# Moving the stores of a streaming rotary-embedding kernel from ScalarE's DMA ring to SyncE's ring of loads, with the later loads placed one slab later

## The chip, the cores and the metric

The kernel runs on one core of one Trainium2 chip. The metric is device microseconds of that core, the median of several executions. A span is the time from the first to the last event of one profiled execution; the reported time is about 2 us longer (162.8 against a span of 160.8 for the kernel before).

## The reference, cut to what matters

```python
batch, seq, dim, num_heads = 16, 512, 1024, 16
x = x.reshape(batch, seq, num_heads, head_dim)            # f32
x1, x2 = x[..., :half_dim], x[..., half_dim:]
rotated = np.concatenate([x1 * cos - x2 * sin,
                          x1 * sin + x2 * cos], axis=-1)  # f32
```

Each element is read once and written once: 33.5 MB in, 33.5 MB out.

## The kernel before

The input is cut into eight slabs of 4 MiB (128 partitions x 8192 f32). Five slab buffers hold loads, and results are written back into the same buffers. A slab is worked on in two halves ("passes"): ScalarE casts a half to bf16 (below: a cast in), VectorE makes two products and a sum, ScalarE casts the result back to f32 in the slab (a cast back), and the finished slab is stored. Loads are issued by SyncE (SP), stores by ScalarE; a DMA ring is the queue of transfers that one of these engines has issued.

```python
def load(s):
    slab[s] = slabs.tile([P, W], f32, tag="slab", name="slab")
    nc.sync.dma_start(out=slab[s], in_=dram(x, s))
...                                   # load(0) to load(4), tables
def cast(u):
    s, k = u
    xb[u] = tpool.tile([P, PW], bf16, tag="xb", name="xb")
    nc.scalar.copy(out=xb[u], in_=view(slab[s], k * PW, (1, PW)))

passes = [(s, k) for s in range(nslabs) for k in range(rpp // rows)]
cast(passes[0])
for i, u in enumerate(passes):
    if i + 1 < len(passes):
        cast(passes[i + 1])           # one pass ahead
    s, k = u
    xs, xu = slab[s], xb.pop(u)
    t2 = t2pool.tile([P, PW], bf16, tag="t2")
    ...                               # VectorE: t2 = xu*sin, xu = xu*cos, xu += swapped t2
    nc.scalar.copy(out=view(xs, k * PW, (1, PW)), in_=xu)
    if k == rpp // rows - 1:
        nc.scalar.dma_start(out=dram(out_flat, s), in_=xs)
        if s + slots < nslabs:
            load(s + slots)
```

The order in this text is not the order on the engines. A scheduler fixes each engine's order when the kernel is built, from its own estimate of when data will be there; the engines then keep to it: in the profile after, ScalarE idles 3.55 us before its cast back at 87.37, although the last packet of slab 5's load had ended at 81.55 and its cast in stands next in the order.

## Time and profile before

| | before |
|---|---|
| time | 162.81 us (162.44 to 162.89) |
| span of the profiled run | 160.8 us |
| ScalarE busy, VectorE busy | 114.8 us, 111.3 us |
| DMA rate over the span | 418 GB/s, 420 to 438 in the stages from 4 to 146.7 us |
| store 7 issued, last byte landed | 146.70, 159.94 us |

In the page's part 2 the span is cut into 40 slices of 4.02 us, and each digit is the busy share of a slice in tenths. A DMA row that is all nines, with engines that are 70% busy, tells that the transfers set the pace. The last slab, in the timeline (columns: start, length, engine, line, operation, and in brackets the idle time before it and what ended it; ACTq and SPq are the engines' DMA issues):

```profile
125.38 3.60 ACT L117 CAST xb<-slab 128x4096 bf16<-128x4096 f32 x1 [5.13 <-DMA slab<-in_x_dram]
128.89 3.60 ACT L137 CAST slab<-xb 128x4096 f32<-128x4096 bf16 x1
...
143.06 3.60 ACT L137 CAST slab<-xb 128x4096 f32<-128x4096 bf16 x1 [3.46 <-DVE xb L133]
146.70 0.34 ACTq L139 DMA_DIRECT2D out_dram<-slab  x1
```

The cast back at 128.89 is slab 6's: ScalarE begins slab 7 before it has finished slab 6.

### The profile page before, as it was taken

What the parts mean: (1) busy time and instruction counts of PE and PEld (TensorE: products, weight loads), DVE (VectorE), ACT (ScalarE), POOL (GpSimd) and SP (SyncE); (2) the same over time, 40 slices, a digit from 0 to 9 for tenths busy, and PEclk for the clock granted to TensorE, in tenths of its full rate; (3) what the DMA queues carried; (4) which work ended last, traced back from release to release, by engine and by line L of the source; (5) the groups of instructions that cost most, each with busy time, mean ns of one, the idle gap of its engine ahead of it and who ended that gap; (6) DMA issues with size and microseconds to landing.
All of it is one profiled execution on the core that took longest, in us unless ns stands there. A gap on an engine that the chain in (4) does not pass through costs nothing.

```text
span 160.8 us, 182 instructions
## 1 busy us (share of the span) xinstructions
PE 0.6 (0%) x4; PEld 0.4 (0%) x4; DVE 111.3 (69%) x52; ACT 114.8 (71%) x33; POOL 2.3 (1%) x9
## 2 busy tenths in 40 slices
PE   0010000000000000000000000000000000000000
PEld 0000000000000000000000000000000000000000
DVE  0003799999999999999997599907997099950000
ACT  3006939899999999999984999069990899744000
POOL 5000000000000000000000000000000000000000
DMA  6999999999999999999999999999999999999993
GB/s 220 448 408 399 473 432 399 473 432 318 416 432 456 408 432 456 416 432 456 416 432 456 416 424 440 440 416 432 456 408 432 465 408 432 456 416 432 456 416 171
DMA packets 2368, 67.24 MB, mean 418 GB/s; under 512 B 288, under 2 KB 288, under 8 KB 320
## 3 DMA queue, kind: packets, MB, share of 16 engines
q1 hardware_dynamic: 1152, 33.55, 49.4%
q10 hardware_dynamic: 1152, 33.55, 48.3%
q0 software_dynamic: 64, 0.13, 0.2%
HBM read 33.69 MB, written 33.55 MB: 418 GB/s over the span
## 4 chain that ended last, share of the span: by engine, by line
DMA 47%; ACT 25%; DVE 13%; issue 6%; ACTq 0%; SPq 0%
DMA slab<-in_x_dram 25%; DMA out_dram<-slab 22%; ACT slab L137 16%; ACT xb L117 9%; DVE xb L133 4%; DVE t L130 4%; DVE xb L130 4%; ACTq L137 0%; SPq L65 0%
## 5 line engine op out<-in xcount | busy, mean ns | idle before, releaser
L117 ACT CAST xb<-slab 128x4096 bf16<-128x4096 f32 x16 | 57.5, 3602 | 27.1 <-DMA slab<-in_x_dram 27.1
L137 ACT CAST slab<-xb 128x4096 f32<-128x4096 bf16 x16 | 57.6, 3603 | 4.1 <-DVE xb L133 3.9
L130 DVE TENSOR_TENSOR t<-xb,tab 128x4096 bf16<-128x4096 bf16 x16 | 36.7, 2291 | 18.8 <-ACT xb L117 18.4
L133 DVE TENSOR_TENSOR xb<-xb,t 128x4096 bf16<-128x4096 bf16 x16 | 36.7, 2292 | 0.5
L130 DVE TENSOR_TENSOR xb<-xb,tab 128x4096 bf16<-128x4096 bf16 x16 | 36.7, 2292 | 0.5
L92 DVE CAST tab<-raw 128x256 bf16<-128x256 f32 x1 | 0.3, 294 | 11.1 <-DMA raw<-in_sin_dram 11.1
L117 ACT ACT_TABLE_LOAD x1 | 1.3, 1283 | 0.7 <-PEq L158 0.7
L102 DVE CAST tab<-acc 128x512 bf16<-128x512 f32 x1 | 0.7, 692 | 0.7 <-PE acc L96 0.7
L75 POOL DMA_DIRECT2D raw<-in_cos_dram x1 | 0.7, 674 | 0.8 <-POOLq L158 0.8
L96 PE MATMUL acc<-tab,pick 128*128 128x128 bf16 x4 | 0.6, 302 | 11.5 <-DVE tab L92 11.5
L87 POOL TENSOR_SCALAR_AFFINE_SELECT pick<-pick 128x128 bf16<-128x128 bf16 x2 | 0.5, 290 | 0.1
L75 POOL DMA_DIRECT2D raw<-in_sin_dram x1 | 0.5, 537 | 0.0
L96 PEld LDWEIGHTS <-pick 128*128 128x128 bf16 x4 | 0.4, 128 | 11.4 <-issue 8.2
L104 DVE CAST tab<-acc 128x256 bf16<-128x256 f32 x1 | 0.4, 416 | 0.0
L106 DVE TENSOR_SCALAR tab<-acc 128x256 bf16<-128x256 f32 x1 | 0.4, 414 | 0.0
L84 POOL MEMSET pick<- 128x256 bf16 x1 | 0.3, 330 | 0.0
L158 POOL MEMSET const-float32-0.0<- 128x1 f32 x1 | 0.1, 100 | 0.2 <-issue 0.2
L158 POOL MEMSET const-bfloat16-1.0<- 128x1 bf16 x1 | 0.1, 103 | 0.0
L158 POOL MEMSET const-uint8-127<- 128x1 uint8 x1 | 0.1, 103 | 0.0
L158 POOL MEMSET const-float32-1.0<- 128x1 f32 x1 | 0.1, 100 | 0.0
## 6 DMA issues: line engine op xcount, KB each, us to landing
slab<-in_x_dram SPq DMA_DIRECT2D x8, 4096.0 KB, 27.1
out_dram<-slab ACTq DMA_DIRECT2D x8, 4096.0 KB, 28.9
raw<-in_cos_dram POOLq DMA_DIRECT2D x1, 64.0 KB, 7.1
raw<-in_sin_dram POOLq DMA_DIRECT2D x1, 64.0 KB, 9.1
```

Of the source, the lines that this page charges most:

```text
L75: nc.gpsimd.dma_start(out=view(raw, i * TR * half, (1, TR * half)), in_=bass.AP(tensor=src.tensor, offset=src.offset, ap=[[TR * half, P], ...
L84: nc.gpsimd.memset(pick, 0.0)
L87: nc.gpsimd.affine_select(out=part, in_=part, compare_op=mybir.AluOpType.not_equal, fill=1.0, base=-g, pattern=[[0, P // SP], [-G, SP]], c ...
L96: nc.tensor.matmul(view(acc, i * TW + g * TR * half, (1, TR * half)), view(pick, g * P, (1, P)), view(tab1, i * TR * half, (1, TR * half)) ...
L102: nc.vector.tensor_copy(out=view(tab, 0, (hd, 2 * rpp), (1, half)), in_=view(acc, 0, (half, 2 * rpp), (1, half)))
L104: nc.vector.tensor_copy(out=view(tab, half, (hd, rpp), (1, half)), in_=view(acc, 0, (half, rpp), (1, half)))
L106: nc.vector.tensor_scalar_mul(out=view(tab, rpp * hd + half, (hd, rpp), (1, half)), in0=view(acc, TW, (half, rpp), (1, half)), scalar1=-1.0)
L117: nc.scalar.copy(out=xb[u], in_=view(slab[s], k * PW, (1, PW)))
L130: nc.vector.tensor_mul(out=t, in0=xu, in1=view(tab, a + k * rows * hd, (hd, rows), (0, nh), (1, hd)))
L133: nc.vector.tensor_add(out=xu, in0=xu, in1=view(t2, half, (hd, rows * nh), (-half, 2), (1, half)))
L137: nc.scalar.copy(out=view(xs, k * PW, (1, PW)), in_=xu)
L158: nc = _bacc.Bacc("TRN2", target_bir_lowering=False, num_devices=1)
```

## The change

The intent is one hardware ring for both directions: five loads, two stores, then a load and a store by turns, then the last stores. As a ring is served in order, a load would never have to share the DMA engines with a store. To make this possible each later load is placed one slab later, so that SyncE, which issues in order, is not held up by a load whose buffer is not yet free.

```diff
         nc.scalar.copy(out=view(xs, k * PW, (1, PW)), in_=xu)
         if k == rpp // rows - 1:
-            nc.scalar.dma_start(out=dram(out_flat, s), in_=xs)
-            if s + slots < nslabs:
-                load(s + slots)
+
+            nc.sync.dma_start(out=dram(out_flat, s), in_=xs)
+            if s >= 1 and s - 1 + slots < nslabs:
+                load(s - 1 + slots)
```

## The prediction

> **What bounds the kernel now.** I first read the page's parts 1 and 2, to see whether an engine or the transfers fill the span. No compute engine does; the DMA engines do.
>
> ```profile
> PE 0.6 (0%) x4; PEld 0.4 (0%) x4; DVE 111.3 (69%) x52; ACT 114.8 (71%) x33; POOL 2.3 (1%) x9
> DMA  6999999999999999999999999999999999999993
> GB/s 220 448 408 399 473 432 399 473 432 318 416 432 456 408 432 456 416 432 456 416 432 456 416 424 440 440 416 432 456 408 432 465 408 432 456 416 432 456 416 171
> HBM read 33.69 MB, written 33.55 MB: 418 GB/s over the span
> ```
>
> Only the first and the last slice (4.02 us each) are not full. The table of windows says the same by stage (columns: window, length, busy time of PE, PEld, DVE, ACT, POOL with counts, clock, DMA share, GB/s):
>
> ```profile
> 4.00:34.40 30.40, 0.59 (x4) 0.32 (x3) 18.81 (x12) 17.85 (x6) 0.00 (x0) 1.00 0.99 428
> 62.80:98.20 35.40, 0.00 (x0) 0.00 (x0) 31.61 (x15) 32.61 (x10) 0.00 (x0) 1.00 1.01 435
> 125.40:146.70 21.30, 0.00 (x0) 0.00 (x0) 13.75 (x6) 17.80 (x5) 0.00 (x0) 1.00 1.02 438
> ```
>
> The first window holds loads alone, the second loads and stores, the third mostly stores. The rate is 428 to 438 GB/s in all, so it depends neither on direction nor on whether one ring or two are active. In the packet records of the trace a 32 KiB packet takes a median of 1.213 us in either queue, and one slab (4 MiB, 8 packets on each of 16 DMA engines) therefore 8 x 1.213 = 9.70 us. Neighbouring loads 1, 2, 3 begin 9.72 and 9.71 us apart, stores 5, 6, 7 9.69 apart: a border between two transfers of one ring costs nothing that can be seen. Sixteen slabs are 155.3 us of a span of 160.8. The kernel before is bound by its transfers, and what compute waits for is mostly them (the list of waits: 27.1 us of ScalarE for loads).
>
> The chain of waits ends in ScalarE's last cast and the last store, but that is not the slack to watch: at 146.7, when store 7 is issued, the ring still held part of store 6, so the DMA engines did not starve. What matters is the timeline of the compute engines, because it says how long they would need without waiting:
>
> ```profile
> 13.50 7.11 ACT L117 CAST xb<-slab 128x4096 bf16<-128x4096 f32 x2 [11.48 <-DMA slab<-in_x_dram]
> 17.14 2.29 DVE L130 TENSOR_TENSOR t<-xb,tab 128x4096 bf16<-128x4096 bf16 x1 [3.67 <-ACT xb L117]
> ...
> 28.39 2.29 DVE L133 TENSOR_TENSOR xb<-xb,t 128x4096 bf16<-128x4096 bf16 x1
> ...
> 30.77 3.60 ACT L137 CAST slab<-xb 128x4096 f32<-128x4096 bf16 x1 [0.45 <-DVE xb L133]
> ...
> 76.82 3.60 ACT L117 CAST xb<-slab 128x4096 bf16<-128x4096 f32 x1
> ...
> 80.33 3.60 ACT L137 CAST slab<-xb 128x4096 f32<-128x4096 bf16 x1
> ...
> 85.11 2.29 DVE L133 TENSOR_TENSOR xb<-xb,t 128x4096 bf16<-128x4096 bf16 x1
> 86.67 3.60 ACT L117 CAST xb<-slab 128x4096 bf16<-128x4096 f32 x1 [2.74 <-DMA slab<-in_x_dram]
> ```
>
> Two rhythms are to be seen. Slab 0 has nothing beside it and runs casts, VectorE, casts back one after the other: 13.50 to 30.77 + 3.60 = 34.37, which is **20.87 us for a slab on its own**. From there to 76.82, ScalarE takes turns (cast in of the next half slab, cast back of this one) and a slab costs 4 x 3.5 = 14.2 us (stores issued at 34.41, 48.59, 62.77, 76.95): **14.18 us for a slab that overlaps its neighbour**.
>
> **What the Trainium skill says.** "DMA: Bandwidth & Descriptors", section "Queues, rings and completion order": SP and ACT each own one row of rings on the same 16 DMA engines, each ring is consumed in order, and an engine goes round the rings packet by packet. The trace agrees: while both queues have work their 32 KiB packets alternate on an engine, each of 1.213 us, and a load that shares takes about 18 us from its first to its last packet where a lone one takes 10.4. Same page, "Issuing engines are not separate DMA queues": issuing from two engines at once saves only sequencer time. The trace agrees here: 428 GB/s with one queue, 435 with two. Same page, "Where 436 GB/s comes from": 435 GB/s as the ceiling; the 428 to 438 measured sit on it, so no ordering can make the transfers themselves faster.
>
> **The change part by part.**
>
> 1. *Removed*: eight store issues of about 0.34 us from ScalarE's queue. In the timeline these lie beside the running cast (ACTq 34.41 within ACT 34.29 to 37.89). Worth nothing.
>
> 2. *Moved*: loads and stores now share one first-in-first-out ring. The total of bytes and the rate stay, so I lay the ring out with 9.71 us for a slab, starting from load 0's landing at 13.48: loads 1 to 4 end at 23.2, 32.9, 42.6, 52.3; then stores 0 and 1 at 62.0 and 71.7; load 5 81.4; store 2 91.1; load 6 100.8; store 3 110.5; load 7 120.2; store 4 129.9; store 5 139.6; store 6 149.3. Is each in the ring by its turn? Load 5 waits for store 0 (62.3) and is due at 71.7. Store 2 is ready at 62.8, due at 81.4. Load 6 waits for store 1 (72.0), due at 91.1; load 7 waits for store 2 (91.5), due at 110.5. SP issues in program order and blocks at each wait, but no block lasts past the due time; the least margin of these is 9 us. Up to here the DMA engines never run dry.
>
> 3. *Moved without being in the diff*: the scheduler has another order on ScalarE. In the built program, loads 5, 6 and 7 are expected late, so from slab 4 on ScalarE no longer takes turns: it has both casts back of slab 4, then both casts in of slab 5, both back of slab 5, both in of slab 6, both back, both in of slab 7, both back. VectorE's order changes with it (t, mul, t, add, mul, add, just that of slab 0). Engines run in program order, so slab 6 cannot start before slab 5 has been cast back, though its data landed long before. Each of slabs 5, 6, 7 now has slab 0's rhythm, 20.87 us in place of 14.18: 3 x 6.7 = **20 us more of compute**, which the before kernel had as waiting for loads instead (first casts after 86.67, 106.03, 125.38).
>
> The compute chain, step by step. Up to ScalarE's 80.33 as before. VectorE's last add of slab 4 ends at 85.11 + 2.29 = 87.40; cast back 87.45 to 91.05; so store 4 is ready at 91.05 (due 120.2). Slab 5's first cast starts at 90.97 (casts follow each other by 3.5 us; its load landed at about 81.7, no wait). Its end: 90.97 + 20.87 = 111.84. Slab 6: from 111.74 to 132.61. Slab 7: from 132.51 to **153.4** (its load landed at 120.5, again no wait). Stores 5 and 6 are ready at 111.8 and 132.6, due at 129.9 and 139.6, in time. **Store 7 is due at 149.3 and ready at 153.4.** The ring is empty for 4 us plus the latency of a cold start.
>
> 4. *The end.* Store 7 starts with an empty ring. The one transfer that did so before, load 0, took 12.74 us from issue to landing (the chain of waits has it as its first DMA piece): 1.0 to the first packet, then slow first packets of 1.8 to 2.1 us, then 1.22 each. A bare 1.0 + 9.7 + 0.35 is 11.1. I take 12.0, an estimate between the two: 153.45 + 12.0 = 165.4. Before, the last landing was 0.9 us ahead of the end of the span (159.9 of 160.8), so the span is 166.3, and the reported time is 2.0 more (162.81 against 160.8): **168.3 us**, that is +5.5 us, or 3.4%. By the same sums, with 11.1 it is 167.4, with 12.74 169.1.
>
> 5. *Given back*: slice 10 of part 2 shows 318 GB/s where its neighbours have about 430, a loss of 4.02 x (1 - 318/430) = 1.05 us just after the first store was issued. Whether the one ring avoids this does not matter: the ring has 4 us to spare before store 7.
>
> **The rivals.**
>
> *A: transfer-bound still, the compute order is hidden.* The full DMA row speaks for it: if the last slab came out before 149.3, the time would be the same sum of bytes, 161.5 to 163. It needs the chain from 91 to 153 to be 4 us shorter. Against it: slab 0's 20.87 us is a measured run of the very same instruction order, and each piece (2.29, 3.60) is constant through the trace.
>
> *B: a change of direction in one ring costs a bubble.* The one dip in slice 10 speaks for it; against it, packets of loads and stores alternate on each DMA engine for 90 us without loss. The new order has seven changes of direction. At 1.05 us each the ring would end store 6 at 156.7 and store 7 at 166.4, in place of 153.4 + 12 = 165.4: about 169.5 in time. Half of it would be hidden in the gap.
>
> *C: faster.* Loads come earlier in the first phase, since no store takes turns with them (load 4 at 52.3). This would help if ScalarE waited for loads in the middle; it has 2.74 + 5.14 + 5.13 us of such waits. But in the new order these turn into waits for VectorE, and the byte sum allows at best 161.
>
> **Range and chances.** The compute chain is deterministic and its sizes are measured, so the doubt is in the last store's cold start (1.6 us) and in B (about 1 us), with 0.5 us either way for how SP and ScalarE hand over. This gives 166.7 to 170.0. Slower by over 2% begins at 166.07, below the range; the chance is 0.93. For A I leave 0.06, for C 0.01.
>
> **What would show it.** In the changed kernel's profile: ScalarE's first casts of slabs 5, 6, 7 at about 91, 112 and 132.5, with none of them waiting for a load; waits of ScalarE for VectorE's add (L133) twice a slab from 91 on; the last cast back ending near 153.4; a nearly empty DMA slice near 150 to 154; one hardware queue with 67 MB; a chain of waits that is ScalarE and VectorE from load 0 to store 7, with one store at its end. I am wrong if ScalarE waits for loads after 91 (then the ring, not the order, sets the end), if the last DMA slices are full (A), or if slices fall to 320 GB/s at each change of direction (B).

## The result, and the profile after

The changed kernel takes **167.59 us** (167.56 to 167.73, 5 runs); the kernel before took 162.81 in the same rounds. The ratio is 1.0301 (95% interval 1.0287 to 1.0315): slower by 3%. A ratio here is the mean time of one kernel's fast runs over that of the other's fast runs of the same rounds, so it is not quite the ratio of the medians quoted.

From the page of the changed kernel, parts 1 to 3 (slices are 4.13 us here):

```profile
PE 0.6 (0%) x4; PEld 0.4 (0%) x4; DVE 110.5 (67%) x52; ACT 114.8 (69%) x33; POOL 2.3 (1%) x9
DMA  7999999899999899998999999999999999990885
GB/s 254 396 396 500 389 460 428 381 500 389 460 428 381 381 484 404 444 444 389 460 420 444 444 412 428 428 444 436 412 428 436 444 436 420 436 420 0 381 381 254
q1 hardware_dynamic: 2304, 67.11, 95.1%
```

The engines do the same work as before. One queue carries all 67.11 MB. What is new is the hole of 0 GB/s in slice 37. The table of windows puts numbers on the end of both kernels (columns: window, length, busy time and counts of PE, PEld, DVE, ACT, POOL, clock, DMA share, GB/s). A packet counts as a whole in the window in which it begins, so a short window can show a share above 1 and a rate above what the ring carries. First the changed kernel:

```profile
144.00:148.00 4.00, 0.00 (x0) 0.00 (x0) 3.96 (x3) 2.83 (x1) 0.00 (x0) 1.00 1.02 442
148.00:150.00 2.00, 0.00 (x0) 0.00 (x0) 1.62 (x1) 1.06 (x2) 0.00 (x0) 1.00 0.31 131
150.00:154.00 4.00, 0.00 (x0) 0.00 (x0) 0.00 (x0) 3.32 (x1) 0.00 (x0) 1.00 0.00 0
154.00:158.00 4.00, 0.00 (x0) 0.00 (x0) 0.00 (x0) 0.00 (x0) 0.00 (x0) 1.00 1.21 516
```

Then the kernel before, same windows:

```profile
144.00:148.00 4.00, 0.00 (x0) 0.00 (x0) 0.00 (x0) 2.67 (x1) 0.00 (x0) 1.00 1.06 459
148.00:150.00 2.00, 0.00 (x0) 0.00 (x0) 0.00 (x0) 0.00 (x0) 0.00 (x0) 1.00 0.91 393
150.00:154.00 4.00, 0.00 (x0) 0.00 (x0) 0.00 (x0) 0.00 (x0) 0.00 (x0) 1.00 1.06 459
154.00:158.00 4.00, 0.00 (x0) 0.00 (x0) 0.00 (x0) 0.00 (x0) 0.00 (x0) 1.00 0.97 418
```

Up to store 6 both kernels have moved the same bytes in the same time: the last packet of store 6 ends at 149.9 us in either trace (the fastest DMA engines are done with it from 148.7). Then the kernel before goes on at once, while the changed one stands still until 154.2, because VectorE and ScalarE are still at slab 7 (their busy columns for 144 to 150 say so). The timeline of the changed kernel shows what they were doing since slab 4:

```profile
76.70 3.60 ACT L117 CAST xb<-slab 128x4096 bf16<-128x4096 f32 x1
...
80.21 3.61 ACT L137 CAST slab<-xb 128x4096 f32<-128x4096 bf16 x1
...
87.37 3.60 ACT L137 CAST slab<-xb 128x4096 f32<-128x4096 bf16 x1 [3.55 <-DVE xb L133]
90.88 7.11 ACT L117 CAST xb<-slab 128x4096 bf16<-128x4096 f32 x2
...
94.51 2.29 DVE L130 TENSOR_TENSOR t<-xb,tab 128x4096 bf16<-128x4096 bf16 x1 [7.23 <-ACT xb L117]
...
103.61 3.60 ACT L137 CAST slab<-xb 128x4096 f32<-128x4096 bf16 x1 [5.63 <-issue]
...
108.15 3.60 ACT L137 CAST slab<-xb 128x4096 f32<-128x4096 bf16 x1 [0.93 <-DVE xb L133]
111.66 7.11 ACT L117 CAST xb<-slab 128x4096 bf16<-128x4096 f32 x2
...
132.44 7.11 ACT L117 CAST xb<-slab 128x4096 bf16<-128x4096 f32 x2
...
149.71 3.60 ACT L137 CAST slab<-xb 128x4096 f32<-128x4096 bf16 x1 [0.94 <-DVE xb L133]
```

From 90.88 on two casts in (x2) follow each other, then ScalarE idles 5.6 us, then come two casts back, and only then the next slab. VectorE in turn idles 7.23 us at each border from one slab to the next. Slabs 5, 6 and 7 start at 90.88, 111.66 and 132.44: 20.78 us each, where a slab cost 14.2 us while casts in and back took turns. No first cast waits for a load. The 5.6 us before 103.61 stand under "issue", though VectorE's sum of that half ended at 101.25 + 2.28 = 103.53, just before: the releaser is inferred and was missed here.

SyncE's part of the same kernel's timeline shows the issues:

```profile
0.74 2.53 SPq L65 DMA_DIRECT2D slab<-in_x_dram  x5
34.29 14.52 SPq L140 DMA_DIRECT2D out_dram<-slab  x2
62.49 0.34 SPq L65 DMA_DIRECT2D slab<-in_x_dram  x1
...
91.89 0.34 SPq L65 DMA_DIRECT2D slab<-in_x_dram  x1
92.32 61.35 SPq L140 DMA_DIRECT2D out_dram<-slab  x4
```

Load 7 is issued at 91.89, long before its turn; the last of four stores ends its issue at 92.32 + 61.35 = 153.67 and takes 0.34, so store 7 was issued at 153.33.

### The profile page after: what moved, and what is told of

It is laid out like the page before. It is cut to its first block, busy times and chain, and to the rows that moved or that the text cites. A ratio compares the mean times of both kernels' runs of the same rounds, so it can differ in the third digit from the quotient of the medians.

```text
span 165.3 us, 193 instructions
## 1 busy us (share of the span) xinstructions
PE 0.6 (0%) x4; PEld 0.4 (0%) x4; DVE 110.5 (67%) x52; ACT 114.8 (69%) x33; POOL 2.3 (1%) x9
## 3 DMA queue, kind: packets, MB, share of 16 engines
q1 hardware_dynamic: 2304, 67.11, 95.1%
```

## The experiments

My theory: the order of casts that the scheduler chose makes compute end at 153.3, after the ring has run dry at 149.9; ring and direction have nothing to do with it. The rivals: one ring for both directions is slower in itself, or the loss is spread over the changes of direction. The pinning used below, `tc.keep_in_program_order(ins)`, holds an instruction behind those written earlier for its engine. `e1` to `e4` ran on one chip in one set of rounds, `e5` to `e7` in another, `e8` in a third, each beside the kernel before. All results are correct but that of `e6`.

**e1: one ring, with turns to the end.** The changed kernel, with both casts pinned to the order of the text.

```diff
-    nc.scalar.copy(out=xb[u], in_=view(slab[s], k * PW, (1, PW)))
+    tc.keep_in_program_order(nc.scalar.copy(out=xb[u], in_=...))
...
-    nc.scalar.copy(out=view(xs, k * PW, (1, PW)), in_=xu)
+    tc.keep_in_program_order(nc.scalar.copy(out=..., in_=xu))
```

> The changed kernel's single ring and issue order are kept; only ScalarE's casts are pinned to the order of the program text, so that it takes turns over slabs 5 to 7 too. My theory (the order of compute costs the time): slab 7 is ready at about 142, before its turn in the ring at 149.8; the DMA engines never run dry and the time falls back to 162.7 us (162.2 to 163.2). Rival (one ring for both directions is itself slower): it stays above 166.

Measured: 162.70 us (4 runs) against 162.86 for the kernel before (7 runs), ratio 0.9989 (0.9963 to 1.0016): the same. The windows of this run (columns as above):

```profile
148.00:150.00 2.00, 0.00 (x0) 0.00 (x0) 0.00 (x0) 0.00 (x0) 0.00 (x0) 1.00 0.88 377
150.00:154.00 4.00, 0.00 (x0) 0.00 (x0) 0.00 (x0) 0.00 (x0) 0.00 (x0) 1.00 1.08 467
154.00:158.00 4.00, 0.00 (x0) 0.00 (x0) 0.00 (x0) 0.00 (x0) 0.00 (x0) 1.00 1.02 442
```

The last line of its timeline for ScalarE:

```profile
138.81 3.60 ACT L137 CAST slab<-xb 128x4096 f32<-128x4096 bf16 x1 [3.42 <-DVE xb L133]
```

Slab 7 is cast back at 142.4, store 7 lies in the ring when its turn comes, and the hole is gone. The ring as such costs nothing, and gains nothing.

**e2: two rings, without turns.** The kernel before, with stores still on ScalarE's ring, but the casts of slabs 5 to 7 put into the changed kernel's order.

```diff
+    def pin(s, ins):
+        if s >= slots - 1:
+            tc.keep_in_program_order(ins)
...                                   # both casts go through pin(s, ...)
-        if i + 1 < len(passes):
+        if u not in xb:
+            cast(u)
+        if i + 1 < len(passes) and (passes[i + 1][0] < slots or passes[i + 1][1]):
             cast(passes[i + 1])
```

> The kernel before with its two rings and its stores issued from ScalarE; only ScalarE's casts of slabs 5 to 7 are pinned to the changed kernel's order (both casts in, both casts back, then the next slab). My theory: the chain 91 + 3 x 20.9 makes store 7 ready at about 153.7 although there are two rings, the time rises to about 167.8 us (167.2 to 168.6). Rival (the ring is the cause, the order is hidden): it stays at 162.8.

Measured: 169.52 us against 162.86, ratio 1.0415 (1.0397 to 1.0433). The order alone brings the loss, with two rings; the rival falls. But it brings 1.7 us more than I expected, outside my range, and this run's timeline tells why:

```profile
91.60 0.34 ACTq L145 DMA_DIRECT2D out_dram<-slab  x1
91.98 7.11 ACT L121 CAST xb<-slab 128x4096 bf16<-128x4096 f32 x2 [0.41 <-ACT slab L143]
...
112.89 0.34 ACTq L145 DMA_DIRECT2D out_dram<-slab  x1
113.27 7.11 ACT L121 CAST xb<-slab 128x4096 bf16<-128x4096 f32 x2 [0.41 <-ACT slab L143]
...
155.47 0.34 ACTq L145 DMA_DIRECT2D out_dram<-slab  x1
```

At each border ScalarE must wait for its own cast back to end, issue the store (0.34 us), and only then begin the next slab. A slab takes 113.27 - 91.98 = 21.29 us in place of 20.78. Three times 0.51, and 0.6 lost on the way to 91.6, make store 7's issue 155.47 - 153.33 = 2.14 us later than in the changed kernel. In the kernel before, the same issue lies beside a running cast.

**e3: the last slab stored in halves.** The changed kernel, all orders kept.

```diff
-        if k == rpp // rows - 1:
+        if s == nslabs - 1:
+            nc.sync.dma_start(out=dram(out_flat, s, k * PW, PW),
+                              in_=view(xs, k * PW, (1, PW)))
+        elif k == rpp // rows - 1:
```

> The changed kernel with slab 7 stored in two halves, each as soon as it is cast back; all orders kept. My theory: only the 4.3 us in which the ring is empty before store 7 are lost. The first half is ready at 148.8, just before the ring drains at 149.8, the second at 153.3, before the first has gone (154.7). So the gap closes and the time is 162.7 us (162.3 to 163.4). Rival (the loss is spread over the whole ring, at each change of direction): at most the wait is halved, about 165.

Measured: 163.53 us, ratio to the kernel before 1.0048 (1.0028 to 1.0068). Four of the 4.8 us are back although compute is as slow as in the changed kernel, so nearly all of the loss sits in that one hole. It is 0.1 above the range I wrote: the first half was issued at 148.92 and its first packet came at 149.76, when the fastest DMA engines had been free since 148.60. I had left out the latency from issue to first packet (0.84 us).

**e4: only the stores moved.** Loads stay where the kernel before has them.

```diff
-            nc.scalar.dma_start(out=dram(out_flat, s), in_=xs)
+            nc.sync.dma_start(out=dram(out_flat, s), in_=xs)
             if s + slots < nslabs:
                 load(s + slots)
```

> Half of the change: stores move to the SP ring, each load is still placed right after the store of its slab as in the kernel before. The built program issues store 0, store 1, load 5, load 6, store 2, store 3, load 7, and ScalarE takes turns between slabs 5 and 6 but not between 4 and 5 or 6 and 7. My theory: the chain loses two of the three overlaps; worked out with 2.3 and 3.6 us it makes slab 7 ready at about 149.4, just ahead of the ring's turn at 149.8, so the time is about 162.8 us (162.3 to 163.8). Rival (a single ring costs in itself): about 167.

Measured: 163.50 us, ratio 1.0045 (1.0026 to 1.0064). Store 7 was issued at 149.29, as worked out (149.4); the same 0.84 us of latency, again left out by me, makes a small hole. With two borders without turns rather than three the loss is nearly gone.

**e5: only the loads placed later.** The other line of the diff, stores on ScalarE.

> The other half of the change: the load is placed one slab later in the program text, stores stay on ScalarE's ring. The built program has the same instructions in the same order on ScalarE and SP as the kernel before. Every theory: 162.8 us (162.4 to 163.2), same; it shows that the later place of the load does nothing by itself.

Measured: 162.87 us against 162.73, ratio 0.9999 (0.9977 to 1.0021): the same. The scheduler's order flips only when stores move.

**e6: the last sum of slab 7 left out** (`if i + 1 < len(passes):` ahead of it).

> The changed kernel without the last VectorE add of slab 7 (a wrong result on purpose in the last half slab). It moves the end of the compute chain forward by 2.3 us and touches no transfer. My theory (the chain sets the end one for one while the ring is empty): 167.6 - 2.3 = 165.3 us (165.0 to 165.6). Rival (the ring sets the end): unchanged at 167.6.

Measured: 166.38 us against 162.73, ratio 1.0215 (1.0198 to 1.0233). Against the changed kernel the span falls from 165.3 to 164.4, that is by 0.9 and not by 2.3 (the median time by 1.2). The direction is right; my size was wrong. This line of its timeline shows it:

```profile
145.28 7.11 ACT L138 CAST slab<-xb 128x4096 f32<-128x4096 bf16 x2 [5.62 <-issue]
```

The two casts back now run without a pause, so ScalarE is the limit from 145.28 on. Only the 0.94 us for which ScalarE had waited before its last cast (the last line of the timeline after) could be won. To take 2.3 us from one engine does not take 2.3 us from a chain that crosses two.

**e7: both remedies**, the edits of e1 and e3 together.

> One ring, ScalarE taking turns to the end, and the last slab stored in halves: both remedies together. My theory: with the DMA engines full there is nothing left to gain, so the time is that of the first remedy alone, 162.6 us (162.2 to 163.0), the same as the kernel before within 0.5%. A rival that one ring is the better carrier and only the order hid it: 161 or less.

Measured: 162.56 us against 162.73, ratio 0.9985 (0.9968 to 1.0002; 7 and 11 runs): the same. With the ring full to the end there is nothing left for a better tail. No version tried beats the kernel before by an amount that can be told from noise.

**e8: one more border without turns.** The changed kernel with the edit of e2, from slab 4 on (`slots - 2` and `slots - 1` in place of `slots - 1` and `slots`).

> The changed kernel with one more border without turns: ScalarE also finishes slab 3 before it begins slab 4, four borders in place of three; one ring and its order are kept. My theory (once the ring is empty, each lost overlap is paid one for one): slab 4 starts at 76.7 and each of slabs 4 to 7 takes 20.8, so store 7 is issued at 160.0 in place of 153.3, lands 11.1 later, and the time is 167.6 + 6.6 = 174.2 us (173.6 to 174.8). Rival (the first three borders cost little and the ring did the rest): 168 to 170.

Measured: 174.02 us against 162.60, ratio 1.0712 (1.0688 to 1.0735). The timeline of this run:

```profile
76.85 7.11 ACT L121 CAST xb<-slab 128x4096 bf16<-128x4096 f32 x2
...
97.63 7.11 ACT L121 CAST xb<-slab 128x4096 bf16<-128x4096 f32 x2
...
139.20 7.11 ACT L121 CAST xb<-slab 128x4096 bf16<-128x4096 f32 x2
```

Slabs are again 20.78 us apart, and the fourth border is paid in full: the spans differ by 172.1 - 165.3 = 6.8 us (6.6 expected), the medians, of different rounds, by 6.4.

All runs in which the ring ran dry before a whole store 7 fit one sum. The store's row in the view by tile gives 11.1 us as the shortest time from issue to landing, in each of them; the end of the span follows 0.9 us later:

| run | store 7 issued | + 11.1 + 0.9 | span measured |
|---|---|---|---|
| e4 | 149.29 | 161.3 | 161.3 |
| e6 | 152.41 | 164.4 | 164.4 |
| changed kernel | 153.33 | 165.3 | 165.3 |
| e2 | 155.47 | 167.5 | 167.4 |
| e8 | 160.1 | 172.1 | 172.1 |

## Why the prediction was right

- *The bound before.* Right. The ring set the time, and e1 with one ring in place of two comes out at the same 162.7. The table in the prediction leaves out the window 34.4 to 62.8, which has the dip of its part 5 and 420 GB/s.
- *Part 1, the issues removed from ScalarE are worth nothing.* Right for the kernel before, where they lie beside casts. It is not a rule: in e2, where no cast is there to cover it, an issue cost 0.51 us.
- *Part 2, the ring never runs dry up to store 6.* Right. Store 6's last packet ended at 149.9 (149.3 forecast). The packet records give the spacing of the transfers: first packets of neighbours are 9.68 to 9.71 us apart at six of the seven changes of direction, and 10.26 at the first one, from load 4 to store 0. First packets show the fastest DMA engine only. In the same records 5 to 10 of the last packets of loads 5, 6 and 7, each followed by a store, took up to 1.57 us in place of 1.21, which is 0.07 to 0.15 us at each of these changes as a mean of the 16 DMA engines. So a change from load to store does cost something here, a tenth of what rival B supposed.
- *Part 3, the order on ScalarE.* Right, and it is the cause: e2 has it with two rings and loses, e1 takes it away with one ring and does not lose, e8 adds a border and pays for it. Slabs 5 to 7 started 20.78 us apart (20.77 in the forecast, whose 20.87 runs from a slab's first cast to the end of its last), and store 7 was issued at 153.33 (153.45 forecast). One sentence of this part is wrong: the kernel before had not all of the 20 us as waiting for loads, but 2.74 + 5.14 + 5.13 = 13.0. The rest is why the chain of compute ends later, at 153.31 in place of 146.66, and of these 6.65 us the ring, busy until 149.9, hides the first part. Two slips in the opening of the prediction did no harm: 4 x 3.5 is 14.0 (the 14.18 is the measured distance of the stores), and slab 0 was not quite alone, as slab 1's first cast lies in it at 23.21.
- *Part 4, the cold start.* The mechanism was right, its size a little off. The term "12.0" measured 11.1: 0.84 to the first packet, 9.9 of packets, 0.35 to landing. This is the bare sum that the prediction gives beside it, partly by luck: its 1.0 and 9.7 are off by 0.2 in opposite directions. Load 0's slow first packets were not those of an empty ring, as packets after the hole took 1.22 us from the start. The 0.9 us too much, less some tenths in the gap between span and time, are the difference of 168.3 and 167.6.
- *Part 5, a dip given back.* It is still there, 10.26 - 9.71 = 0.55 us, and stayed hidden. That one ring makes it smaller is not shown: the packets around the first store took in sum, per DMA engine, 1.0 us more than 1.213 each in the kernel before and 0.7 in the changed one, but also only 0.7 and 0.6 in `e2` and `e5`, which have two rings.
- *Rivals.* A did not happen here, but e4 shows how near it was: with store 7 ready 4 us sooner the time is 163.5. B fell with the spacing above and with e1: what a change costs is far below 1.05 us. C fell with e1 and e7, where loads come early, turns are kept and nothing is won.
- *What the profile was to show.* The first casts are at 90.88, 111.66 and 132.44 with no wait for a load, the hole is at 150 to 154, one queue has 67 MB. Two signs came out otherwise: of ScalarE's two waits a slab for VectorE the list has one as "issue", and the page's chain of waits goes back only to 136 us in place of reaching load 0. Neither speaks of the cause; the timeline has both.

What the scheduler's reason was for the new order is not shown by any run. That it depends on the stores' place is: e5 built the same order as before, e4 two of the three borders.

## What to carry to other kernels

When a change moves a transfer, compare the built order of instructions on every engine, also on those that the diff does not touch: here the order by itself cost 4.8 us with one ring and 6.7 us (`e2`) with two. A transfer-bound kernel hides slack in compute, but only up to the last transfer: work out when the last store is ready and when its turn comes, with the latency from issue to first packet on the store's side. If an experiment is to shorten a chain, check first how long the next engine in it is busy without the piece taken out.

## What the Trainium skill lacked or had wrong

- "DMA: Bandwidth & Descriptors" has no cost for a change of direction within one ring. Here it was 0.55 us at the first store of the program; at the later changes the first packets of 4 MiB transfers stayed 9.68 to 9.71 us apart, as between transfers of one direction, and slower last packets of a load before a store came to 0.07 to 0.15 us at a change. With two rings, the rate of one slice fell to 318 GB/s after the first store was issued, a loss of 1.05 us. No run here shows the cause.
- The same page, section "Issuing engines are not separate DMA queues", calls the issue time usually small beside the transfer, which agrees with 0.34 us beside 9.7. It gives no cost for an issue on a compute engine that has no other work to cover it: in e2 that was 0.51 us per slab on the critical path.
- The same page fits the duration of a DMA for the GpSimd path only, as 2.0 us and bytes over 436 GB/s, which for 4 MiB makes 11.6 us (an estimate from that fit). For the path from SP and ACT it has a first-byte latency of about 0.6 us, but no such fit. A single 4 MiB store issued from SP or ACT into an empty ring took 11.1 us from issue to landing in five kernels; in the changed kernel 0.84 us of it lay between the start of the issue and the first packet.
